# The engines' order around the context's last rows written out by hand, the transposes placed between the first products of two pairs, and the second matrix's sums put two pairs later

## The chip, the cores and the metric

One core of one Trainium2 chip runs the whole program. The metric is the device time of one execution in microseconds (us), given as the median over several runs.

## The reference

One layer of a backbone for 256 context tokens and 1024 latent tokens, model width 1024, in float32. The part that matters here is its second half, computed for both kinds of tokens:

```python
    x = x + gt1 * (merged @ w_out)
    u2 = rmsnorm(x, g_norm2) * (1 + sc2) + sh2
    x = x + gt2 * (jnp.square(jax.nn.relu(u2 @ w_ff1)) @ w_ff2)
```

`gt1`, `sc2`, `sh2` and `gt2` come from the conditioning vector (one for context tokens, one for latent ones), and `w_ff1` is 1024 x 4096, `w_ff2` 4096 x 1024.

## The kernel before, in words

All numbers are float32. A product of two float32 matrices is made of three matmuls: each operand is split into a high part, which ScalarE casts, and a low part, the rest, which VectorE subtracts; then high by high, low by high and high by low are summed in PSUM. Names that end in `h` and `l` (or begin with `hi_` and `lo_`) are these parts.

The tokens stand in tiles of 128: 0 to 3 are the first group of latent tokens (512), 4 to 7 the second, 8 and 9 the context (256). The steps around the change are:

- **The output projection.** `project_out(tiles, c0, n, ...)` multiplies `merged` by a stretch of `n` columns of `w_out`, 24 matmuls for a tile, and leaves the sum in a PSUM tile `po{c0}_{tile}`. VectorE multiplies it by `gt1` and adds it to x; ScalarE squares x and gathers the row sums in `fsq`. The context's tiles 8 and 9 go by quarters of 256 columns: `context_out(0)` to `context_out(3)`, with weights from `context_weights(q)` (tiles `hi_wc`, `lo_wc`).
- **The normalization.** `modulate_ff(g)` takes a group's row sums (`fs`), makes the reciprocal root (`rstd_of`: a small step on VectorE, then one on GpSimd, `rs_f`), scales x by it (tiles `xn`, the even ones on ScalarE, the odd ones on VectorE), transposes on TensorE into a PSUM tile (`pt2{g}_{k}`) and applies scale and shift on ScalarE. For groups 0 and 1 the result is `u2r{k}_{g}`, with its split `u2h`, `u2l`; for the context (g = 2) it goes back into the PSUM tile, and VectorE makes the split `u2{k}c` from it. These PSUM tiles share one pool of five (`ps_sd`) with the results of the products below.
- **The first matrix.** The 4096 columns of `w_ff1` are worked off in 16 pairs. For the latent tokens a pair is a 2 x 2 block product in the way of Strassen and Winograd, with seven products of 12 matmuls of 128x512 each. `begin()` splits two of the four weight quarters (`a11`, `a12`) and makes the first two products, `B11` and `B21` (PSUM `fB11_{pair}`, `fB21_{pair}`): ScalarE copies the first one twice, VectorE adds the second, and `done` is relu and square on ScalarE. `contexts()` makes the plain products for the context tokens (PSUM `fc{pair}`) with all four weight quarters. `rest()` makes the other five products (`T4`, `T2`, `T3`, `T1`, `B22`; PSUM `fT...`), whose operands are sums: on the side of the tokens `quarter_sums`, four subtractions for each of four rows, and their splits `split_sum`, both made once; on the side of the weights four sums for each pair, with the splits `s1` to `s4`. `sums()` stores the results.
- **The second matrix's sums.** `second_sums(fp)` loads a pair's block of `w_ff2` (SyncE's queue), makes four subtractions of 128x512 on GpSimd (L1242) and stores them in `scr_t`. The product with the second matrix, behind all 16 pairs, loads them from there.

The 16 latent transposed tiles of 128x512, `u2r0` to `u2r7` for two groups, are the operands of the products. Pairs 0 and 1 share `slot` tiles for their weights: `a21_0` goes into the room of `a11_0`, `a21_1` into that of `a11_1`, and so on, which sets when the later quarter can be split.

What sets the order: the program's text gives the instructions, and a scheduler with a timeline of its own reorders each engine's instructions when the program is built, within their dependencies; loads are reordered on SyncE's queue as well. An instruction that is issued through `Pinned` keeps its place in the written order among the pinned ones of its engine. On the chip each engine works off its instructions strictly in the built order. Before the change nothing in this part is pinned. Instructions issued through `Pinned` carry L43, the line of the wrapper.

The written order before is: `context_out(0)`, `context_out(1)`, `modulate_ff(1)`, `context_out(2)`, `context_out(3)`, then `begin()` of pairs 0 and 1, `modulate_ff(2)`, `quarter_sums`, the four `split_sum`, `contexts()` of both pairs, and for each pair its remaining steps with `second_sums` of the same pair at the end.

Of the kernel before, what the change touches and what calls it, by code (L numbers as in the profile page):

```python
# [48 lines left out]
def hybrid_step(  # L49
# [77 lines left out]
    def rstd_of(ssq, n, name):  # L127
        r = small([P, 16], f"rs_{name}")
        V.tensor_scalar(r[:, :n], ssq, 1.0 / n_of[name[0]], EPS, ALU.mult, ALU.add)  # L129
        G.tensor_tensor(r[:, :n], r[:, :n], neghalf[:, :n], ALU.pow)  # L130
        return r
# [738 lines left out]
    def split(raw, name, room=ring):  # L870
        hi, lo = room(f"{name}h"), room(f"{name}l")
        A.copy(hi, raw)
        V.tensor_tensor(lo, raw, hi.bitcast(F32), ALU.subtract)
# [20 lines left out]
    class Pair:  # L894
# [23 lines left out]

        def begin(self):
            a11, a12, a21, a22 = self.raw  # L920
            self.w11 = split(a11, f"a11_{self.name}", self.rooms[0])
            ps = self.prod(self.w11, "B11")
            A.copy(self.a1, ps)
            A.copy(self.a2, ps)
# [2 lines left out]
            V.tensor_tensor(self.a1, self.a1, ps, ALU.add)
# [317 lines left out]

# [290 lines left out]
```

## Time and profile before

| | |
|---|---|
| median of 3 runs | 1947.19 us (1946.92 to 1949.57) |
| profiled execution | 1947.31 us |
| its span in the trace | 1945.5 us, 28129 instructions |
| mean granted TensorE clock | 0.994 |
| TensorE busy | 1903.0 us, 98% of the span |
| VectorE, ScalarE, GpSimd busy | 1294.0, 861.7 and 378.2 us |
| chain that ended last | TensorE 87%, VectorE 4%, transfers 3%, GpSimd 2% |

Times of the trace are counted from the start of the span. A row of the timeline gives the start, the duration, the engine, the line, the operation, its output and its inputs with their shapes, the count of such instructions in one piece, and in square brackets the idle time ahead with the instruction that ended it. TensorE's matmuls overlap at their ends, so what one costs is the distance to the start of the next; the same holds, by less, for VectorE and ScalarE. In the trace buffer numbers are left out (`fB` stands for `fB11_0` and the others, `a_0l` for the low part of a weight quarter of pair 0), and which is meant follows from the order.

### The profile page before, as it was taken

What the parts mean: (1) busy time and instruction counts of PE and PEld (TensorE: products, weight loads), DVE (VectorE), ACT (ScalarE), POOL (GpSimd) and SP (SyncE); (2) the same over time, 40 slices, a digit from 0 to 9 for tenths busy, and PEclk for the clock granted to TensorE, in tenths of its full rate; (3) what the DMA queues carried; (4) which work ended last, traced back from release to release, by engine and by line L of the source; (5) the groups of instructions that cost most, each with busy time, mean ns of one, the idle gap of its engine ahead of it and who ended that gap; (6) DMA issues with size and microseconds to landing.
All of it is one profiled execution on the core that took longest, in us unless ns stands there. A gap on an engine that the chain in (4) does not pass through costs nothing.

```text
span 1945.5 us, 28129 instructions
## 1 busy us (share of the span) xinstructions
PE 1903.0 (98%) x10136; PEld 1627.5 (84%) x10136; DVE 1294.0 (67%) x2207; ACT 861.7 (44%) x1768; POOL 378.2 (19%) x380
## 2 busy tenths in 40 slices
PE   6999999999999999999999999999999999999998
PEld 3778888998788888888888887888888888888886
DVE  6574443347759889875675599888776655744665
ACT  7444464653243333343123374555454545443443
POOL 1200001107302424220000015444431110000003
PEclk9999999999999999999999999999999999999999
DMA  9211111012635445469522435776773586654444
GB/s 361 85 59 33 43 39 40 27 56 70 203 119 165 149 158 164 153 211 321 163 97 98 152 120 212 253 264 246 259 269 136 193 333 203 210 170 151 165 133 159
DMA packets 149318, 313.32 MB, mean 161 GB/s; under 512 B 17550, under 2 KB 40818, under 8 KB 147130
## 3 DMA queue, kind: packets, MB, share of 16 engines
q1 hardware_dynamic: 107354, 220.73, 33.9%
q0 software_dynamic: 15520, 57.75, 7.8%
q10 hardware_dynamic: 26304, 33.04, 4.7%
q8 instruction: 79, 1.29, 0.3%
q14 instruction: 61, 0.50, 0.1%
HBM read 217.59 MB, written 93.36 MB: 160 GB/s over the span
## 4 chain that ended last, share of the span: by engine, by line
PE 87%; DVE 4%; DMA 3%; POOL 2%; ACT 1%; issue 1%; SPq 0%; POOLq 0%; ACTq 0%; DVEq 0%
PE w L1403 6%; PE w L1404 6%; PE w L1405 6%; PE pb L1050 3%; PE pb L1051 3%; PE pb L1052 3%; PE fT L892 3%; PE fT L890 3%; PE fT L891 3%; PE fB L891 2%; PE fB L890 2%; PE fB L892 2%; PE fT_g L892 2%; PE fT_g L890 2%; PE fT_g L891 2%; PE po L1168 2%
## 5 line engine op out<-in xcount | busy, mean ns | idle before, releaser
L1242 POOL TENSOR_TENSOR z<-z 128x512 f32<-128x512 f32 x64 | 100.1, 1564 | 123.3 <-DMA z<-in_w_ff 120.6
L947 DVE TENSOR_TENSOR z<-z 128x512 f32<-128x512 f32 x112 | 88.7, 792 | 2.5
L527 POOL PARTITION_ALL_REDUCE acc<-acc x16 | 54.6, 3446 | 184.0 <-DVE acc L521 113.6
L521 DVE SCALAR_TENSOR_TENSOR acc<-z,scond,acc 128x512 f32<-128x512 f32 x112 | 86.1, 816 | 0.0
L1357 POOL TENSOR_TENSOR rs_y<-rs_y,neghalf 128x1 f32<-128x1 f32 x10 | 9.6, 966 | 333.0 <-DVE rs_y L1356 333.0
L1208 ACT ACTIVATE z<-z 128x512 f32<-128x512 f32 x64 | 40.5, 632 | 69.8 <-DVE z L956 36.7
L972 ACT ACTIVATE z<-z 128x512 f32<-128x512 f32 x48 | 30.3, 632 | 59.1 <-DVE z L956 23.1
L130 POOL TENSOR_TENSOR rs_h<-rs_h,neghalf 128x4 f32<-128x4 f32 (+1 forms) x12 | 10.9, 910 | 200.5 <-DVE rs_h L129 200.3
L653 DVE SCALAR_TENSOR_TENSOR yc<-th,ccol,z 128x512 f32<-128x512 f32 (+1 forms) x12 | 7.9, 661 | 58.2 <-PE th L651 58.2
L1056 DVE TENSOR_TENSOR sg<-pb,sg 128x512 f32<-128x512 f32 (+1 forms) x48 | 28.7, 600 | 26.7 <-PE pb L1052 26.5
L881 ACT CAST hi_wb<-raw_wb 128x512 fp32r<-128x512 f32 x24 | 14.8, 620 | 64.4 <-PE pb L1051 37.6
L1209 ACT ACTIVATE z<-z 128x512 f32<-128x512 f32 x64 | 40.3, 629 | 1.1
L1171 DVE TENSOR_TENSOR po<-po,gt 128x512 f32<-128x512 f32 (+1 forms) x24 | 14.6, 607 | 35.1 <-PE po L1170 35.0
L1233 POOL DMA_DIRECT2D scr_s<-x x48 | 26.3, 549 | 53.1 <-DVE x L1227 47.6
L738 POOL TENSOR_TENSOR z<-z 128x1024 f32<-128x1024 f32 (+13 forms) x20 | 33.6, 1702 | 6.9 <-ACT z L722 4.6
L528 POOL TENSOR_TENSOR acc<-acc,bt 1x512 f32<-1x512 f32 x16 | 23.5, 1480 | 58.4 <-issue 58.4
L1174 ACT ACTIVATE po<-z 128x512 f32<-128x512 f32 (+1 forms) x24 | 12.7, 529 | 48.5 <-DVE z L1173 34.2
L587 DVE SCALAR_TENSOR_TENSOR z<-z,dmb,kv 128x129 f32<-128x129 f32 x56 | 16.6, 345 | 21.8 <-PE kv L576 21.3
L1057 DVE TENSOR_TENSOR z<-z,sg 128x512 f32<-128x512 f32 (+1 forms) x48 | 28.7, 601 | 1.2
L640 DVE TENSOR_TENSOR den<-den,gcol 128x2 f32<-128x2 f32 x40 | 6.2, 159 | 31.0 <-ACT den L639 29.9
L43 PE MATMUL pm<-wah,shl 128*4 128x512 f32 x32 | 13.8, 461 | 13.2 <-ACT wah L43 13.2
L130 POOL TENSOR_TENSOR rs_f<-rs_f,neghalf 128x4 f32<-128x4 f32 (+1 forms) x3 | 3.3, 1092 | 116.9 <-DVE rs_f L129 116.9
(5136 smaller groups left out, 7288.9 us busy)
## 6 DMA issues: line engine op xcount, KB each, us to landing
z<-in_w_ff SPq DMA_DIRECT2D x64, 512.0 KB, 5.5
z<-in_w_ada SPq DMA_DIRECT2D x64, 256.0 KB, 3.1
scr_t<-z POOLq DMA_DIRECT2D x16, 1024.0 KB, 4.9
z<-in_w_in SPq DMA_DIRECT2D x24, 512.0 KB, 4.3
scr_g<-z ACTq DMA_DIRECT2D x48, 256.0 KB, 2.0
sg<-scr_g SPq DMA_DIRECT2D x48, 256.0 KB, 4.5
scr_h<-z ACTq DMA_DIRECT2D x48, 256.0 KB, 3.6
scr_s<-x POOLq DMA_DIRECT2D x48, 256.0 KB, 4.3
```

The lines of the kernel that those rows point to most:

```text
L521: V.scalar_tensor_tensor(acc[j], raw, scond[:, k, j : j + 1], acc[j], ALU.mult, ALU.add)
L890: PE.matmul(ps, whi[:, s], ahi, start=first and k == ks[0], stop=False)
L891: PE.matmul(ps, whi[:, s], alo, start=False, stop=False)
L892: PE.matmul(ps, wlo[:, s], ahi, start=False, stop=end and k == ks[-1])
L947: V.tensor_tensor(out, x, y, op)
L1050: PE.matmul(pb[:, :n], whi[:, s], yh, start=kc == 0, stop=False)
L1051: PE.matmul(pb[:, :n], whi[:, s], yl, start=False, stop=False)
L1052: PE.matmul(pb[:, :n], wlo[:, s], yh, start=False, stop=kc == 3)
L1242: G.tensor_tensor(out, x, y, ALU.subtract)
L1403: PE.matmul(banks[j], h_[:, s], rh, start=fp == 0, stop=False)
L1404: PE.matmul(banks[j], l_[:, s], rh, start=False, stop=False)
L1405: PE.matmul(banks[j], h_[:, s], rl, start=False, stop=fp == NFP - 1)
```

## The change

1. `context_out(2)`, `context_out(3)` and all that follows up to the split of the sums is issued through `Pinned`: VectorE, ScalarE, GpSimd and TensorE keep the written order. The weights of both quarters, the feeds of the pairs 0 and 1 and their splits are issued ahead or between, unpinned.
2. `begin()` is cut into `split_first`, `first` and `second`, and `modulate_ff` into `root_ff` and the quarters to be done. The written order now is: first product of pair 0, second product of pair 0, first quarter of the context's rows (transposes `pt22_0`, `pt22_1`), first product of pair 1, second quarter, second product of pair 1, and the last two quarters.
3. The rows of `quarter_sums` (now `row_sums(kk)`) stand one by one among these steps, pinned on VectorE. The split sums are pinned on VectorE as well, in the order T4, T2, T3, T1.
4. SyncE's loads of the pair loop are pinned, and `second_sums` of a pair is written behind the steps of the pair two later; the last two stand behind the loop.
5. In the product with the second matrix, the order of the places that take the first raw loads (`FREE`) changes.

```diff
+        def first(self):
+            ps = self.prod(self.w11, "B11")
+            A.copy(self.a1, ps)
+            A.copy(self.a2, ps)
+
+        def second(self):
+            ps = self.prod(self.w12, "B21")
+            V.tensor_tensor(self.a1, self.a1, ps, ALU.add)
+            self.done(self.a1)
...
+    def row_sums(kk):
+        b11, b21, b12, b22 = (raw2q[nm][kk] for nm in ("B11", "B21", "B12", "B22"))
+        for out, x, y in ((b11, b12, b11), (b12, b22, b12), (b22, b22, b11), (b21, b22, b21)):
+            V.tensor_tensor(out, x, y, ALU.subtract)
...
     for fp in (0, 1):
         feed_pair(fp)
-        pairs[fp].begin()
-    modulate_ff(2)
-    quarter_sums(raw2q)
-    for nm in ("T4", "T3", "T2", "T1"):
+    wcs = [context_weights(q) for q in (2, 3)]
+    V, A, G, PE = (Pinned(tc, e) for e in engines)
+    context_out(2, wcs[0])
+    row_sums(0)
+    context_out(3, wcs[1])
+    P4, (V, A, G, PE) = (V, A, G, PE), engines
+    for fp in (0, 1):
+        pairs[fp].split_first()
+    V, A, G, PE = P4
+    rc = root_ff(2)
+    row_sums(1)
+    pairs[0].first()
+    pairs[0].second()
+    modulate_ff(2, rc, (0,))
+    pairs[1].first()
+    modulate_ff(2, rc, (1,))
+    row_sums(2)
+    pairs[1].second()
+    modulate_ff(2, rc, (2, 3))
+    A, G, PE = engines[1:]
+    row_sums(3)
+    for nm in ("T4", "T2", "T3", "T1"):
         split_sum(u2s, raw2q, nm)
+    V = engines[0]
     for fp in (0, 1):
         pairs[fp].contexts()
+    SP = Pinned(tc, nc.sync)
     for fp in range(NFP):
...
         del pairs[fp]
-        second_sums(fp)
+
+        if fp > 1:
+            second_sums(fp - 2)
+    second_sums(NFP - 2)
+    second_sums(NFP - 1)
+    SP = nc.sync
...
-    FREE = (0, 2, 16, 18, 12, 14, 4, 6, 8, 10)
+    FREE = (0, 2, 12, 14, 16, 18, 4, 6, 8, 10)
```

Three places of the built order show what moves.

**The front, on TensorE.** Between the second and the third quarter of the context's projection stand the transposes of `modulate_ff(1)`; `pt21_{k}` is transposed tile k of the second latent group, `xn4` and `xn6` are its even tiles of scaled rows by quarter. Before, its tile 6 stands among the last matmuls of `po512_8`:

```order
L1170 MATMUL po512_8_10722<-lo_wc2_3_10719,m6c_9782 128x256
L1168 MATMUL po512_8_10722<-hi_wc2_3_10718,m7c_9785 128x256
L1142 MATMUL pt21_6_10676<-cst_76,xn4_3_10670 128x128 x2
L1169 MATMUL po512_8_10722<-hi_wc2_3_10718,m7c_9785 128x256
L1170 MATMUL po512_8_10722<-lo_wc2_3_10719,m7c_9785 128x256
L1142 MATMUL pt21_6_10676<-cst_76,xn6_3_10673 128x128 x2
L1168 MATMUL po512_9_10750<-hi_wc2_0_10700,m0c_9764 128x256
```

After the change tiles 5, 6 and 7 stand with the others, ahead of the first matmul of `po512_8`:

```order
L1158 MATMUL pt21_5_10659<-cst_76,xn4_2_10642 128x128 x2
L1158 MATMUL pt21_5_10659<-cst_76,xn6_2_10645 128x128 x2
L1158 MATMUL pt21_6_10676<-cst_76,xn4_3_10670 128x128 x2
L1158 MATMUL pt21_6_10676<-cst_76,xn6_3_10673 128x128 x2
L1158 MATMUL pt21_7_10687<-cst_76,xn4_3_10670 128x128 x2
L1158 MATMUL pt21_7_10687<-cst_76,xn6_3_10673 128x128 x2
L43 MATMUL po512_8_10806<-hi_wc2_0_10760,m0c_9764 128x256 x2
```

What moved is the last three tiles' transposes: all of them now come before the third quarter's first product.

**The context's first quarter, on ScalarE and VectorE.** `fB11_0`, `fB21_0` and `fB11_1`, `fB21_1` are the first two products of pairs 0 and 1, `xn8_{q}` the scaled context rows by quarter, and the `z` rows between are the copies, relu and square of a pair. ScalarE before:

```order
L923 COPY z_74<-fB11_1_10963 128x512
L924 COPY z_74<-fB11_1_10963 128x512
L1174 ACTIVATE po768_8_10802,fsq_9815<-z_74 128x256
L1174 ACTIVATE po768_9_10831,fsq_9815<-z_74 128x256
L1208 ACTIVATE z_74<-z_74 128x512
L1209 ACTIVATE z_74<-z_74 128x512
L1221 DMA scr_h0_10860<-z_74 128x512
L1208 ACTIVATE z_74<-z_74 128x512
L1209 ACTIVATE z_74<-z_74 128x512
L1221 DMA scr_h1_10861<-z_74 128x512
L1134 ACTIVATE xn8_0_11003<-z_74,rs_f2_11000 128x256
L1134 ACTIVATE xn8_1_11020<-z_74,rs_f2_11000 128x256
```

ScalarE after:

```order
L43 ACTIVATE po768_8_10866,fsq_9815<-z_74 128x256
L43 COPY z_74<-fB11_0_10949 128x512 x2
L43 ACTIVATE po768_9_10895,fsq_9815<-z_74 128x256
L43 ACTIVATE z_74<-z_74 128x512 x2
L43 ACTIVATE xn8_0_10980<-z_74,rs_f2_10942 128x256
L1234 DMA scr_h0_10698<-z_74 128x512
L43 ACTIVATE pt22_0_10983<-pt22_0_10983,sh2_9799,a2_9798 128x256
L43 ACTIVATE pt22_1_10990<-pt22_1_10990,sh2_9799,a2_9798 128x256
L43 COPY z_74<-fB11_1_10997 128x512 x2
L43 ACTIVATE xn8_1_11012<-z_74,rs_f2_10942 128x256
L43 ACTIVATE pt22_2_11015<-pt22_2_11015,sh2_9799,a2_9798 128x256
L43 ACTIVATE pt22_3_11022<-pt22_3_11022,sh2_9799,a2_9798 128x256
```

The first quarter `xn8_0` now stands behind relu and square of pair 0 alone and ahead of the copies of pair 1's first product; before, all four quarters stood behind both pairs. VectorE before:

```order
L927 TENSOR_TENSOR z_74<-z_74,fB21_0_10941 128x512
L780 TENSOR_TENSOR u2r6_0_10333<-u2r6_1_10681,u2r6_0_10333 128x512
L790 TENSOR_TENSOR t2l2_11128<-u2r6_1_10681,t2h2_11127 128x512
L780 TENSOR_TENSOR u2r7_1_10692<-u2r7_1_10692,u2r3_0_10288 128x512
L1122 TENSOR_REDUCE fs2_10998<-fsq_9815 128x2
L927 TENSOR_TENSOR z_74<-z_74,fB21_1_10982 128x512
L780 TENSOR_TENSOR u2r7_0_10344<-u2r7_1_10692,u2r7_0_10344 128x512
L129 TENSOR_SCALAR rs_f2_11000<-fs2_10998 128x2
L1136 TENSOR_SCALAR xn8_0_11003<-z_74,rs_f2_11000 128x256
```

VectorE after:

```order
L43 TENSOR_REDUCE fs2_10940<-fsq_9815 128x2
L43 TENSOR_SCALAR rs_f2_10942<-fs2_10940 128x2
L43 TENSOR_TENSOR u2r1_0_10260<-u2r1_1_10620,u2r1_0_10260 128x512
L43 TENSOR_TENSOR u2r1_1_10620<-u2r5_1_10664,u2r1_1_10620 128x512
L43 TENSOR_TENSOR u2r5_1_10664<-u2r5_1_10664,u2r1_0_10260 128x512
L43 TENSOR_TENSOR u2r5_0_10316<-u2r5_1_10664,u2r5_0_10316 128x512
L43 TENSOR_TENSOR z_74<-z_74,fB21_0_10964 128x512
L43 TENSOR_SCALAR xn8_0_10980<-z_74,rs_f2_10942 128x256
```

Before, the row sums that lie around the small steps `fs2` and `rs_f2` are the last rows of the quarter sums; now row 1 as a whole stands between `rs_f2` and the addition of `fB21_0`, and rows 2 and 3 come later. On TensorE `pt22_0` and `pt22_1` now follow the last matmul of `fB21_0`, with `fB11_1` behind them; before, `pt22_0` followed `fB21_1`.

**Pair 1's second product and the context's third quarter, on ScalarE.** `a21_0h` is the high part of pair 0's third weight quarter, `pt22_{k}` the scale and shift of a transposed context tile, `T4h0` the first split of the sums. Before:

```order
L1146 ACTIVATE pt22_5_11047<-pt22_5_11047,sh2_9799,a2_9798 128x256
L1146 ACTIVATE pt22_6_11057<-pt22_6_11057,sh2_9799,a2_9798 128x256
L1146 ACTIVATE pt22_7_11064<-pt22_7_11064,sh2_9799,a2_9798 128x256
L789 CAST T4h0_11087<-u2r4_0_10305 128x512
L872 CAST a21_0h_11179<-z_74 128x512
L789 CAST T4h1_11091<-u2r5_0_10316 128x512
```

After:

```order
L43 ACTIVATE pt22_3_11022<-pt22_3_11022,sh2_9799,a2_9798 128x256
L872 CAST a21_0h_11179<-z_74 128x512
L43 ACTIVATE z_74<-z_74 128x512 x2
L43 ACTIVATE xn8_2_11049<-z_74,rs_f2_10942 128x256
L1234 DMA scr_h1_10699<-z_74 128x512
L43 ACTIVATE pt22_4_11052<-pt22_4_11052,sh2_9799,a2_9798 128x256
L43 ACTIVATE pt22_5_11059<-pt22_5_11059,sh2_9799,a2_9798 128x256
```

`a21_0h` stood behind all eight context tiles; now it stands ahead of relu and square of pair 1 and of `xn8_2`.

More of the change, by code (lines that the diff above doesn't have):

```diff
@@ L917, in context, with split_first @@
                 self.context_done(self.hc[:, f * 256 : f * 256 + 256], o)
+        def split_first(self):
+            a11, a12, a21, a22 = self.raw
+            self.w11 = split(a11, f"a11_{self.name}", self.rooms[0])
+            self.w12 = split(a12, f"a12_{self.name}", self.rooms[1])
+        def first(self):
[6 more added lines that the diff above has]
+            self.done(self.a1)
         def begin(self):
@@ L921, in begin @@
             self.w11 = split(a11, f"a11_{self.name}", self.rooms[0])
-            ps = self.prod(self.w11, "B11")
-            A.copy(self.a1, ps)
-            A.copy(self.a2, ps)
+            self.first()
             self.w12 = split(a12, f"a12_{self.name}", self.rooms[1])
-            ps = self.prod(self.w12, "B21")
-            V.tensor_tensor(self.a1, self.a1, ps, ALU.add)
-            self.done(self.a1)
+            self.second()
         def contexts(self):
@@ L1116, in hybrid_step, with root_ff @@
     fsq = cp.tile([P, NT, 4], F32, name="fsq")
-    def modulate_ff(g):
+    def root_ff(g):
         t0, n = GROUPS[g]
@@ L1122, in modulate_ff @@
         V.reduce_sum(fs, fsq[:, tiles[0] : tiles[-1] + 1, 0 : 4 if g == 2 else 2], axis=mybir.AxisListType.X)
-        r = rstd_of(fs, len(tiles), f"f{g}")
+        return rstd_of(fs, len(tiles), f"f{g}")
+    def modulate_ff(g, r=None, quarters=range(4)):
+        t0, n = GROUPS[g]
+        tiles = range(t0 // P, (t0 + n) // P)
+        r = root_ff(g) if r is None else r
         j = 1 if g == 2 else 0
-        for qt in range(4):
+        for qt in quarters:
             xn = []
@@ L1176, in project_out, with context_out @@
                 SP.dma_start(scr_x[i], xt[i])
-    def context_out(q):
-        ws = context_weights(q)
+    def context_out(q, ws):
         project_out((8, 9), q * 256, 256, lambda k: tuple(w[:, k % 2 * 256 : k % 2 * 256 + 256] for w in ws[k // 2]))
@@ L1188, in hybrid_step @@
     project_out(range(5, 8), 512, 512, lambda k: w_out1[k])
-    context_out(0)
-    context_out(1)
+    for q in (0, 1):
+        context_out(q, context_weights(q))
     modulate_ff(1)
@@ L1193, in hybrid_step @@
     raw2q = {nm: raw2[g][o : o + 4] for nm, g, o in quarters}
-    context_out(2)
-    context_out(3)
     NFP = NFF // 2
```

## The prediction

> **What bounds the kernel now.** I read the first lines of the page, then TensorE's own waits from 1080 to 1620 us (the stretch that the diff touches), then busy time by stretch.
>
> ```profile
> span 1945.5 us, 28129 instructions
> PE 1903.0 (98%) x10136; PEld 1627.5 (84%) x10136; DVE 1294.0 (67%) x2207; ACT 861.7 (44%) x1768; POOL 378.2 (19%) x380
> PE pt L1142 <- ACT xn L1134: 3.0, 1, 3.0
> PE fT L890 <- ACT s_0h L872: 0.9, 3, 0.4
> PE fT L892 <- DVE s_2l L873: 0.9, 1, 0.9
> PE fc L890 <- ACT hc L1212: 0.7, 1, 0.7
> PE fT L890 <- ACT s_2h L872: 0.7, 1, 0.7
> PE w L1403 <- ACT r_13h L1302: 0.5, 1, 0.5
> 1150.00:1160.00 10.00, 6.97 (x31) 5.58 (x30) 8.24 (x19) 6.35 (x15) 0.70 (x1) 0.94 0.39 158
> 1170.00:1180.00 10.00, 8.94 (x59) 7.61 (x57) 10.00 (x18) 7.01 (x16) 2.50 (x3) 1.00 0.64 228
> 1210.00:1220.00 10.00, 9.22 (x51) 7.34 (x49) 7.15 (x14) 5.06 (x10) 2.62 (x5) 1.00 0.97 345
> 1220.00:1230.00 10.00, 8.43 (x51) 7.22 (x50) 9.93 (x13) 5.27 (x12) 7.79 (x8) 1.00 0.62 221
> 1230.00:1560.00 330.00, 330.00 (x1746) 285.31 (x1745) 246.49 (x364) 169.57 (x314) 118.33 (x135) 1.00 0.65 233
> ```
>
> TensorE works in 1903.0 of 1945.5 us, so it is the bound. A wait row is what waited, for whom, the sum, the count and the longest. The six rows come to 6.7 us: the change can hardly win more here than that and the little lost at a low clock. In the window rows (span, then PE, PEld, DVE, ACT, POOL, granted clock, DMA share) TensorE is full from 1230 on, and VectorE is full from 1170 to 1180. Here VectorE is a second bound, and whatever makes VectorE idle before 1190 comes out again as TensorE's wait.
>
> The one large wait, 3.0 us, is for `xn8_0`, the normalized last context rows. Its chain:
>
> ```profile
> 1153.88 0.59 ACT L924 COPY z<-fB 128x512 f32<-128x512 f32 x1
> 1154.77 0.39 ACT L1174 ACTIVATE po<-z 128x256 f32<-128x256 f32 x1
> 1155.17 0.62 ACT L1208 ACTIVATE z<-z 128x512 f32<-128x512 f32 x1
> 1155.83 0.63 ACT L1209 ACTIVATE z<-z 128x512 f32<-128x512 f32 x1
> 1158.56 1.71 ACT L1134 ACTIVATE xn<-z,rs_f 128x256 f32<-128x256 f32 x4 [0.40 <-POOL rs_f L130]
> 1156.12 0.69 DVE L927 TENSOR_TENSOR z<-z,fB 128x512 f32<-128x512 f32 x1 [0.38 <-PE fB L892]
> 1156.72 0.68 DVE L780 TENSOR_TENSOR u2r<-u2r,u2r 128x512 f32<-128x512 f32 x1
> 1157.33 0.16 DVE L129 TENSOR_SCALAR rs_f<-fs 128x2 f32<-128x2 f32 x1
> 1157.57 0.70 POOL L130 TENSOR_TENSOR rs_f<-rs_f,neghalf 128x2 f32<-128x2 f32 x1 [33.16 <-DVE rs_f L129]
> 1145.01 0.40 PE L890 MATMUL fB<-u2h,a_0h 128*128 128x512 f32 x1
> 1155.69 0.39 PE L892 MATMUL fB<-u2h,a_1l 128*128 128x512 f32 x1
> 1159.12 2.39 PE L1142 MATMUL pt<-cst,xn 128*128 128x128 f32 x10 [3.03 <-ACT xn L1134]
> ```
>
> All four first products of pairs 0 and 1 run together from 1145.01 to 1155.92 (48 matmuls between these two rows, 0.227 apart, so 2.73 a product). TensorE idles 3.03 us, and only then come the transposes.
>
> **The change, part by part: the front.** Before, the last three transposed tiles of `modulate_ff(1)` lie among the projection's matmuls; now they all stand ahead of `po512_8`.
>
> ```profile
> 1130.03 2.35 PE L1142 MATMUL pt<-cst,xn 128*128 128x128 f32 x20
> 1132.13 0.36 PE L1168 MATMUL po<-hi_wc,m0c 128*128 128x256 f32 x1
> 1134.40 0.78 ACT L1151 ACTIVATE u2r<-pt,sh,a 128x512 f32<-128x512 f32 x1
> 1144.77 0.28 PE L1169 MATMUL po<-hi_wc,m7c 128*128 128x256 f32 x1
> 1144.89 0.28 PE L1170 MATMUL po<-lo_wc,m7c 128*128 128x256 f32 x1
> ```
>
> Twenty transposes take 2.10 (1130.03 to 1132.13), four 0.35 or so. They fill the five tiles at hand; the last three wait until ScalarE has emptied tiles, the third with `u2r2`, which ends at 1135.18. So `po512_8` starts at about 1135.6, not 1132.13. Then its four products of 24 matmuls, 0.12 apart (1144.77, 1144.89), run undisturbed: 11.5 us, to 1147.1. Before it was 1145.01: **+2.1**.
>
> **First stall.** Pair 0's two products end at 1147.1 + 5.45 = 1152.6, and TensorE's next instruction is `pt22_0`, which needs `xn8_0`. By the rows above: `fB11_0` is in at 1150.1; two copies at 0.48 (0.59 with the end) to 1151.1; the square of `po768_9`, on which the row sum depends, 0.5 to 1151.6; the reduction and `rs_f2` 0.3 to 1151.9; GpSimd's 0.70 to 1152.7. VectorE meanwhile has `row_sums(1)`, four at 0.60 (1156.72 to 1157.33 is one such step), written ahead of the addition of `fB21_0`: to 1154.4. The addition ends at 1155.1, relu and square (0.66 each, 1155.17 to 1155.83) at 1156.4, and only behind these on ScalarE stands `xn8_0`, at 0.4: 1156.8. TensorE idles 4.2. It then stands at 1156.85 with two products of four done; the other two at 5.45 make it equal to 1162.3 of before, where this point was 1159.12: **a lag of 3.2**.
>
> **Second stall.**
>
> ```profile
> 1168.15 0.62 ACT L872 CAST a_0h<-z 128x512 fp32r<-128x512 f32 x1 [0.56 <-PE fc L891]
> ```
>
> `pt22_0`, `pt22_1` 0.4, `fB11_1` 2.73, twelve context matmuls 1.44: 1161.4. `xn8_1` stands behind the two copies of `fB11_1` (1161.6), `pt22_2`, `pt22_3` to 1162.0, `fB21_1` to 1164.8, twelve matmuls to 1166.25. `pt22_4` needs `xn8_2`, which on ScalarE stands behind `a21_0h`, relu and square of pair 1. The new wait is that of `a21_0h`: it overwrites `a11_0h`, which TensorE's context products of `u23c` read until 1166.0. Before, such a cast had the same wait, 0.56 (1168.15), but stood behind everything on ScalarE that made `xn8`. Behind it now: the cast 0.62 to 1166.65; on VectorE `a21_0l` and the last of `row_sums(2)` at 0.60, and the addition, to 1168.6; relu, square and `xn8_2` to 1170.45. TensorE idles 4.2 again. Without the wait at `a21_0h` the addition starts at 1164.9, `xn8_2` is ready at about 1167.4, and this stall is 1.1; so that one wait is worth 3.
>
> **Behind it.**
>
> ```profile
> 1163.50 0.54 ACT L1146 ACTIVATE pt<-pt,sh,a 128x256 f32<-128x256 f32 x1 [0.40 <-PE pt L1142]
> 1164.82 0.41 DVE L1147 CAST u26c<-pt 128x256 fp32r<-128x256 f32 x1
> 1180.95 0.68 DVE L873 TENSOR_TENSOR s_0l<-z,s_0h 128x512 fp32r<-128x512 f32 x1
> 1181.69 0.50 PE L892 MATMUL fT<-t2h,s_0l 128*128 128x512 f32 x1 [0.30 <-DVE s_0l L873]
> 1167.52 1.77 DVE L873 TENSOR_TENSOR a_0l<-z,a_0h 128x512 fp32r<-128x512 f32 x1
> 1164.37 6.08 POOL L1242 TENSOR_TENSOR z<-z 128x512 f32<-128x512 f32 x4 [6.10 <-DMA z<-in_w_ff]
> 1178.57 13.34 POOL L1242 TENSOR_TENSOR z<-z 128x512 f32<-128x512 f32 x4 [7.20 <-DMA z<-in_w_ff]
> ```
>
> VectorE and ScalarE set the pace: `pt22_4` takes 0.4 on TensorE and 0.54 on ScalarE, to 1171.4; the cast and the dependent subtraction of `u24c` on VectorE end at 1172.05, those of `u25c` at 1172.85 (each 0.41); VectorE's half of `xn8_3` 0.33, transposes and ScalarE again to 1173.95; `u26c` 1174.8, `u27c` 1175.6. Then 22 operations at 0.60 and two short ones up to `s2_0l`, 13.6: it ends at about 1189.3. Before, its counterpart ended at 1181.63 (1180.95 and 0.68), and TensorE ran the matmul on it at 1181.69: **a lag of 7.7**. The late `second_sums` have their gain in this already: while GpSimd subtracts, VectorE's 128x512 operations take up to 1.77 (1167.52) where alone they take 0.68 (1180.95), about 3 us lost in the 6.08 from 1164 alone, an estimate from two such operations and three more behind them. The walk has none of this. If GpSimd's work had stayed, the lag would be 3 more.
>
> **Clock.**
>
> ```profile
> 1160.00:1161.00 1.00, 1.00 (x7) 1.00 (x6) 0.29 (x1) 1.00 (x3) 0.00 (x0) 0.50 0.29 82
> 1163.00:1164.00 1.00, 1.00 (x11) 1.00 (x10) 1.00 (x4) 0.60 (x2) 0.00 (x0) 1.00 0.60 246
> ```
>
> The granted clock falls to 0.50 after the idle 3.03 us and is back by 1163; the ten transposes then take 2.07 (1159.12 to the next matmul) instead of 1.05. Two idles of 4.2 can each do the same. Behind the first stands a whole product, so about 1.5 us are lost there; behind the second little, since VectorE sets the pace. Between 0 and 3 for both; I take 1.2, near the one loss that this trace shows. [...]
>
> **Behind 1192.** The second sums now run two pairs late and SyncE's loads are pinned in their written order. The three later waits (`s_2h`, `hc`, `s_2l`: 2.3 together, the gaps of the windows from 1210 to 1230) lie behind GpSimd's and SyncE's work, which the change moves. Bounds: all three go (-2.3) or none does and `a11_2h` comes late in the pinned queue (+1). I take -1.2. From 1230 on TensorE has no gap in 330 us to give, so neither late sums nor the order of `FREE` can win there; what they can touch behind that stretch is the 0.5 at `r_13h`, which may go or grow: 0, plus or minus 1.
>
> **Sum.** 7.7 + 1.2 - 1.2 = +7.7 on the profiled execution's 1947.31 (the span and 1.8 around it; the median of the runs is 1947.19, the same within 0.01%): **1955.0 us**.
>
> **Rivals.** 0.2%, 3.9 us, is about what a measurement of this kernel can tell from no change, so faster is below 1943.3 and slower above 1951.1.
> - *The transposes are hidden: faster, 1939 to 1943.* This holds if `xn8_0` is ready when `fB21_0` ends (1152.6) and `xn8_2` when the context's twelve matmuls end. Then the 3.03 idle, the 1.5 of clock and up to 2.3 behind go, against the front's +2.1: 1947.3 - 6.8 + 2.1 = 1942.6, or 1940.5 if the front's 2.1 is taken up by the wait that goes. For it: GpSimd's losses do go. Against it: four row sums and a relu and a square stand ahead of `xn8_0`; it decides at 1152.6, and my walk misses it by 4. Chance 0.17.
> - *The lag is caught up: 1946 to 1951.* If the wait at `a21_0h` is short (the cast finds its room free), the second stall is 1.1, the lag falls to 4.7, and the later waits go: 1947.3 + 4.7 - 2.3 = 1949.7. Chance 0.13.
> - *Worse than the walk: 1958 to 1963.* Both stalls cost a half clock at full price (+3) and pair 2's weights come late in the pinned queue (+1 to +2) with none of the later waits gone: 1947.3 + 7.7 + 3 + 1.5 = 1959.5. Chance 0.15.
> - *The pins don't hold the order:* the built order shows them in place, so I give this nothing.
>
> **How the numbers follow.** The walk has 0.55, by itself 1951 to 1958; with the worse case, slower has 0.70, same 0.13, faster 0.17. The range goes from 1942.0 to 1961.0: the deeper half of the hidden case and the far end of the worse one, some 0.15 together, are left out.
>
> **What would show it.** Right: two TensorE waits on `pt22_0` and `pt22_4` of about 4 us each, `po512_8` some 3.5 us later than before, an idle VectorE from 1155 to 1175, and 1.77 gone from its 128x512 operations up to 1195. Wrong: transposes that follow `fB21_0` without a gap; a short wait at `a21_0h`; or a gap behind 1230 that the first stage does not explain.

## The result, and the profile after

| | before | after |
|---|---|---|
| median of 4 runs each | 1948.38 us (1946.92 to 1950.46) | 1967.57 us (1965.55 to 1969.30) |
| profiled execution, its span | 1947.31, 1945.5 us | 1967.77, 1966.0 us |
| mean granted TensorE clock | 0.994 | 0.992 |
| chain that ended last: TensorE, VectorE, transfers | 87%, 4%, 3% | 81%, 7%, 5% |

The ratio after to before is 1.0097, with a 95% interval from 1.0085 to 1.0109: the change makes the kernel slower by 1%. The predicted 1955.0 us has the right sign, but the time lies above the range that ended at 1961.0.

The first question is where the 20.5 us of span came from. The two executions reach the changed stretch 0.6 us apart, so I divide the span at two marks: the first of the transposes of `modulate_ff(1)`, and the first matmul on `w`, with which the product with the second matrix begins. TensorE's timeline gives them, the changed kernel's first:

```profile
1130.60 2.78 PE L1158 MATMUL pt<-cst,xn 128*128 128x128 f32 x24
1567.62 0.50 PE L1447 MATMUL w<-r_0h,l_0h 128*128 128x512 f32 x1
```

and the second mark of before (its first mark, 1130.03, stands in the prediction):

```profile
1556.23 0.39 PE L1403 MATMUL w<-r_0h,l_0h 128*128 128x512 f32 x1
```

From mark to mark (stage A: the last context rows and the 16 pairs) it is 437.0 us instead of 426.2, so 10.8 more. From the second mark to the end (stage B: the second matrix) it is 1966.0 - 1567.62 = 398.4 instead of 389.3, so 9.1 more. The remaining 0.6 lies ahead of both. **About half of the loss thus lies in a stage for which the prediction had 0, plus or minus 1.**

The largest of TensorE's waits of the changed kernel from 1080 to 1640 us (what waited, for whom, sum, count, longest) and all of `w` show both halves:

```profile
PE pt L43 <- ACT xn L43: 8.5, 3, 4.3
PE w L1447 <- ACT r_13h L1346: 2.0, 1, 2.0
PE w L1447 <- ACT accU L1411: 1.6, 1, 1.6
PE w L1447 <- ACT l_4h L1346: 1.5, 1, 1.5
PE w L1448 <- DVE c_0l L1347: 0.5, 1, 0.5
PE w L1447 <- ACT r_12h L1346: 0.3, 1, 0.3
```

The wait for `xn` has grown from 3.0 to 8.5, and five waits of `w` with 5.9 us stand where before there was one of 0.5. The busy time by stretch of the same kernel (span, then PE, PEld, DVE, ACT and POOL busy, granted clock, DMA share, GB/s):

```profile
1150.00:1160.00 10.00, 5.66 (x22) 4.47 (x21) 5.66 (x14) 4.50 (x11) 1.07 (x1) 0.86 0.33 132
1160.00:1170.00 10.00, 8.61 (x49) 7.23 (x47) 5.15 (x11) 3.09 (x6) 0.00 (x0) 0.97 0.00 0
1170.00:1180.00 10.00, 5.70 (x27) 4.90 (x28) 4.58 (x12) 4.60 (x9) 0.00 (x0) 0.66 0.07 26
1190.00:1200.00 10.00, 7.53 (x23) 5.09 (x23) 10.00 (x20) 5.57 (x11) 0.57 (x1) 0.83 0.09 26
1210.00:1560.00 350.00, 350.00 (x1859) 302.83 (x1858) 284.87 (x389) 176.44 (x328) 141.70 (x150) 1.00 0.63 233
1600.00:1605.00 5.00, 2.64 (x9) 1.04 (x8) 3.72 (x7) 3.21 (x6) 0.00 (x0) 0.93 0.91 344
1605.00:1610.00 5.00, 5.00 (x18) 4.04 (x18) 4.44 (x8) 4.73 (x9) 1.08 (x2) 0.72 0.65 206
```

In the stretches from 1150 to 1180 VectorE, ScalarE and GpSimd idle together with TensorE: nobody is short of time there, each waits for the next in a chain. From 1190 to 1200 VectorE is full: it works off what was put back. From 1210 to 1560 TensorE is full again. Behind 1600, in stage B, it loses 2.4 us, and its clock falls for some 3 us (0.72 from 1605 to 1610).

The two stalls, on TensorE's timeline:

```profile
1157.43 1.11 PE L43 MATMUL pt<-cst,xn 128*128 128x128 f32 x4 [4.34 <-ACT xn L43]
1172.77 1.11 PE L43 MATMUL pt<-cst,xn 128*128 128x128 f32 x4 [4.00 <-ACT xn L43]
1174.54 0.58 PE L890 MATMUL fc<-u24c,a_0h 128*128 128x256 f32 x1 [0.66 <-DVE u24c L43]
1177.48 0.59 PE L43 MATMUL pt<-cst,xn 128*128 128x128 f32 x3
1194.57 0.66 PE L892 MATMUL fT<-t2h,s_0l 128*128 128x512 f32 x1 [0.74 <-DVE s_0l L873]
```

They are 4.34 and 4.00 us long, where the prediction had 4.2 and 4.2, and what VectorE and ScalarE did ahead of the second one is what it said: `a_0h` waits for TensorE, and addition, relu, square and `xn` follow it one after the other. The cast on ScalarE:

```profile
1168.45 0.62 ACT L872 CAST a_0h<-z 128x512 fp32r<-128x512 f32 x1 [3.07 <-PE fc L891]
```

### The profile page after: what moved, and what is told of

Its sections match the earlier page's. It is cut to its first block, busy times and chain, and to the rows that moved or that the text cites. A ratio compares the mean times of both kernels' runs of the same rounds, so it can differ in the third digit from the quotient of the medians.

```text
span 1966.0 us, 28101 instructions
## 1 busy us (share of the span) xinstructions
PE 1910.3 (97%) x10136; PEld 1630.4 (83%) x10136; DVE 1314.3 (67%) x2207; ACT 861.8 (44%) x1768; POOL 378.7 (19%) x380
## 4 chain that ended last, share of the span: by engine, by line
PE 81%; DVE 7%; DMA 5%; ACT 3%; issue 2%; POOL 1%; SPq 0%; POOLq 0%; DVEq 0%; ACTq 0%
PE w L1447 5%; PE w L1449 5%; PE w L1448 5%; PE fT L892 3%; PE fT L890 3%; PE fT L891 3%; PE pb L1062 3%; PE pb L1061 3%; PE pb L1063 3%; PE fB L891 2%; PE fB L892 2%; PE fB L890 2%; PE po L1184 2%; PE po L1185 2%; PE po L1186 2%
## 5 line engine op out<-in xcount | busy, mean ns | idle before, releaser
L958 DVE TENSOR_TENSOR z<-z 128x512 f32<-128x512 f32 x112 | 110.8, 989 | 2.5
L1244 POOL DMA_DIRECT2D scr_c<-xc x16 | 11.6, 726 | 131.5 <-DVE xc L1243 131.5
```

The lines of the kernel that those rows point to most:

```text
L958: V.tensor_tensor(out, x, y, op)
```

## The experiments

Every table entry comes from its kernel's profiled execution, except the ratio, which compares the runs with those of before on the same chip (95% interval in brackets). The forecasts call the kernels by names: experiments 1 to 12 are there e1, e2, e3, e5, e7, e6, e8, e9, e13, e12, e14 and e15.

| kernel | stage A | stage B | ratio |
|---|---|---|---|
| before | 426.2 | 389.3 | 1 |
| the change | 437.0 | 398.4 | 1.0097 [1.0085, 1.0109] |
| 1: order by hand, sums as before | 450.1 | 389.5 | 1.0111 [1.0089, 1.0133] |
| 2: late sums, order as before | 419.9 | 397.4 | 1.0005 [0.9994, 1.0016] |
| 3: 1 with `a21_0` behind | 450.9 | 389.9 | 1.0117 [1.0102, 1.0132] |
| 4: 3 with the rows first | 446.7 | 393.6 | 1.0102 [1.0081, 1.0123] |
| 5: the change, front as before | 435.2 | 396.5 | 1.0079 [1.0060, 1.0099] |
| 6: 2 with sums that catch up | 419.9 | 389.5 | 0.9968 [0.9956, 0.9980] |
| 7: the change, all rows early | 422.5 | 397.3 | 1.0022 [1.0012, 1.0032] |
| 8: 7 with sums that catch up | 423.8 | 390.6 | 0.9984 [0.9974, 0.9994] |
| 9: the change with sums that catch up | 437.2 | 389.4 | 1.0046 [1.0030, 1.0062] |
| 10: 8 with three steps moved | 426.4 | 389.4 | 1.0001 [0.9992, 1.0010] |
| 11: 6 again | 421.0 | 389.3 | 0.9961 [0.9948, 0.9975] |
| 12: the change, other places | 436.3 | 400.8 | 1.0107 [1.0085, 1.0128] |

Stage B takes 389.3 to 390.6 in every kernel whose last second sums are done early, but for the fourth, and 396.5 to 400.8 in every kernel where they are late. In stage A the sixth kernel differs from its own repeat by 1.1 (419.9 and 421.0): behind the same stall of 3.0 us the clock was halved for about 3.4 us in the sixth and for about 6.8 in the repeat, an estimate from windows of 10 us (from 1150 and from 1160 the clock is 0.99 and 0.83 in the sixth, 0.87 and 0.79 in the repeat). So a difference of about 1 us in this table is not read as an effect.

**1 and 2: the change in its two halves.** The first keeps the order by hand and puts the second sums back:

```diff
-    SP = Pinned(tc, nc.sync)
     for fp in range(NFP):
...
-        if fp > 1:
-            second_sums(fp - 2)
-    second_sums(NFP - 2)
-    second_sums(NFP - 1)
-    SP = nc.sync
+        second_sums(fp)
...
-    FREE = (0, 2, 12, 14, 16, 18, 4, 6, 8, 10)
+    FREE = (0, 2, 16, 18, 12, 14, 4, 6, 8, 10)
```

> The hand-written order of the change alone; the second matrix's sums, SyncE's order and FREE as before. Theory A (two separate losses: the order costs about 12 between 1130 and 1200, the late sums cost about 9 at the start of the second matrix's product): 1957 to 1960 us, stalls of about 4 at pt22_0 and pt22_4 as in the change, and the waits behind 1560 (5.9 us) gone. Theory B (the late sums cost nothing, as the prediction had it; the waits behind 1560 come from the late arrival out of the first stage): 1965 to 1968 us with those waits still there.

The second is before with only the late sums, the pinned loads and the new `FREE` (the same lines the other way).

> The kernel before, with only the sums two pairs late, SyncE pinned in the pair loop and the new FREE. Theory A: 1953 to 1957 us, waits of 5 to 8 us in the product w, none new between 1130 and 1560, VectorE free of GpSimd between 1164 and 1191. Theory B: 1945 to 1949 us.

The first took 1972.80 us, more than either theory gave, and through a wait that neither had. Among its TensorE waits, and then SyncE's largest wait from 1150 to 1240:

```profile
PE fc L890 <- ACT a_2h L872: 6.9, 1, 6.9
```

```profile
SPq L1252 <- DMA scr_t<-z: 28.6, 3, 13.6
```

and SyncE's queue, where L1252 are the loads of the second sums and L905 those of the pairs' weights:

```profile
1202.55 0.33 SPq L905 DMA_DIRECT2D z<-in_w_ff  x1
1216.59 0.80 SPq L1252 DMA_DIRECT2D z<-in_w_ff  x2
1217.45 11.77 SPq L905 DMA_DIRECT2D z<-in_w_ff  x3
```

Its window from 1160 to 1240 (columns as above):

```profile
1160.00:1240.00 80.00, 64.53 (x281) 52.25 (x281) 59.41 (x97) 35.70 (x69) 33.30 (x22) 0.82 0.43 154
```

The same stretch of the changed kernel, of before and of the second experiment, in this order:

```profile
1160.00:1240.00 80.00, 71.48 (x364) 60.02 (x363) 66.09 (x109) 41.71 (x81) 19.43 (x21) 0.93 0.38 140
```

```profile
1160.00:1240.00 80.00, 75.56 (x397) 63.22 (x396) 74.12 (x113) 43.83 (x85) 39.39 (x31) 0.99 0.63 226
```

```profile
1160.00:1240.00 80.00, 79.56 (x431) 69.12 (x430) 69.47 (x116) 48.29 (x93) 25.51 (x26) 0.98 0.52 180
```

The order by hand makes TensorE idle for 15.5 us of these 80 and lowers its clock (0.82 over these 80, 0.54 from 1220 to 1230). Pair 2's first weight load goes out at 1202.55, about when it does in the changed kernel (1201.56). Its second one, which `a_2h` needs, goes out only at 1217.45: on the queue it stands behind two loads of the second sums, and the first of these waited 13.6 us until a store of earlier sums had freed its place. With the late sums the idle time falls to 8.5, in the old order from 4.4 to 0.4. In stage A the late sums win 13.1 us in the new order (450.1 to 437.0) and 6.3 in the old one (426.2 to 419.9); the order by hand costs 23.9 without them and 17.1 with them. "Late sums" is a bundle here: the sums come two pairs later and SyncE's loads are pinned. Which of the two wins in stage A, no run parted. In the second experiment the waits in stage B appear at once (2.0 at `r_13h`, 1.1 at `l_4h`, 0.8 at `r_4h`, 0.7 at `r_12h`; 4.6 together, and a clock of 0.91 from 1560 to 1600), stage B is 8.1 longer, and its 1950.99 us is no change.

**3 and 4: which wait makes the second stall.** The prediction held that the wait of `a21_0h` is worth 3 us. The third kernel pins its split behind the last context rows, on top of the first:

```diff
     modulate_ff(2, rc, (2, 3))
+    pairs[0].w21 = split(pairs[0].raw[2], "a21_0", pairs[0].rooms[2])
     A, G, PE = engines[1:]
```

> As e1, but the split of a21_0 stands behind pt22_7 on ScalarE and VectorE. If the wait of a21_0h makes the second stall: pt22_4's stall falls from 4.0 to about 1 and the time is 3 to 5 us under e1. If VectorE's pace sets the end of this stretch whatever TensorE does: the stall goes but the time is within 1 us of e1.

The second stall fell from 4.00 to 3.03, and the time stayed (1974.12 us). The wait was worth 1, not 3: with the cast gone, the four steps of `row_sums(2)` still stand ahead of the addition on VectorE.

The fourth puts the first quarter's rows ahead of `row_sums(1)`, the addition and relu, and the last two ahead of pair 1's addition:

```diff
-    row_sums(1)
     pairs[0].first()
-    pairs[0].second()
+    pairs[0].second_product()
     modulate_ff(2, rc, (0,))
+    row_sums(1)
+    pairs[0].second_done()
     pairs[1].first()
     modulate_ff(2, rc, (1,))
     row_sums(2)
-    pairs[1].second()
+    pairs[1].second_product()
     modulate_ff(2, rc, (2, 3))
+    pairs[1].second_done()
```

> As e3, and the context's quarters stand ahead of row_sums(1) and ahead of addition, relu and square of their pair, behind the products on TensorE. If what stands ahead of xn8_0 makes the first stall: pt22_0's stall falls from 4.3 to about 1, no half clock follows, and the time is 1945 to 1951 us. If the transposes between the products are no better than behind them (VectorE's pace): within 2 us of e3.

TensorE's timeline of it:

```profile
1152.61 0.66 PE L43 MATMUL pt<-cst,xn 128*128 128x128 f32 x4 [0.57 <-ACT xn L43]
1161.45 1.11 PE L43 MATMUL pt<-cst,xn 128*128 128x128 f32 x4 [4.02 <-ACT xn L43]
```

The stall at `pt22_0` falls from 4.34 to 0.57, so the steps written ahead of `xn8_0` made it. But one quarter later the same stall stands at `pt22_2`, since the row sums, the addition, relu, square and two copies now lie ahead of `xn8_1`. It was moved, not removed (1970.69 us). Stage B has 4 us more here than the others with early sums; 2.4 of it is a wait for the eviction `accU`, whose cause I did not follow.

**5: the front.** The third quarter's projection is not pinned on TensorE:

```diff
     V, A, G, PE = (Pinned(tc, e) for e in engines)
+    P4, PE = (V, A, G, PE), engines[3]
     context_out(2, wcs[0])
+    PE = P4[3]
```

> The whole change, but context_out(2) is not pinned on TensorE, so that the last transposes of modulate_ff(1) may lie among its matmuls again. If the front's loss of 2.1 is carried to the end: 1965 to 1966 us (2 under the change). If the stalls behind it take it up: within 0.7 of the change, 1967 to 1968.

Stage A is 1.8 shorter (437.0 to 435.2), where the prediction priced the front at 2.1. The 1.9 that stage B and the 0.4 that the part ahead of the marks have less are not the front's. The median, 1963.84 us, is 3.7 below the change's and so below both forecasts, by that shorter stage B, whose cause is open.

**6 and 11: are the late sums late at the end?** The second experiment, but with sums that lag at first and catch up by pair 13:

```diff
-        if fp > 1:
-            second_sums(fp - 2)
-    second_sums(NFP - 2)
-    second_sums(NFP - 1)
+        for s in {2: (0,), 3: (1,), 4: (2,), 5: (3, 4), 6: (5,), 7: (6, 7), 8: (8,), 9: (9, 10),
+                  10: (11,), 11: (12, 13), 12: (14,), 13: (15,)}.get(fp, ()):
+            second_sums(s)
```

> As e2 (the order of before, sums late), but the sums catch up: from pair 5 on every second pair issues two, so that the last stands behind pair 13. Theory C (what the late sums lose in the product w is that the last two sums still hold the places of its first raw loads): w begins at about 1550 as in e2, its waits fall from 4.6 us and a half clock to under 1, 1940 to 1943 us. Rival (the pinned loads or the new FREE delay w, not the lateness): 1946 to 1951 us with the waits still there.

1943.17 us: the gain in stage A stays (419.9) and the loss in stage B is gone (389.5). The pinned loads and the new `FREE` are those of the second, so in stage B it was the lateness that cost. Its TensorE waits of the whole stretch are three:

```profile
PE pt L1142 <- ACT xn L1134: 3.0, 1, 3.0
PE w L1407 <- ACT r_13h L1306: 0.6, 1, 0.6
PE fT L890 <- ACT a_0h L872: 0.4, 1, 0.4
```

This is the fastest version of the study. It was run once more (experiment 11):

> e6 again, unchanged, beside e12 on the same chip: 1940 to 1944 us.

It gave 1941.43 us, a ratio of 0.9961.

**7 and 8: transposes between the products, without the stalls.** On top of the fifth, all four quarters of `xn8` come right behind the root, ahead of pair 0's addition; the transposes stand behind the third product and among the context's products, and `a21_0` behind them. The eighth adds the sums that catch up.

```diff
     pairs[0].first()
-    pairs[0].second()
-    modulate_ff(2, rc, (0,))
+    pairs[0].second_product()
+    rows = scaled_rows(rc)
+    pairs[0].second_done()
+    row_sums(1)
     pairs[1].first()
-    modulate_ff(2, rc, (1,))
-    row_sums(2)
-    pairs[1].second()
-    modulate_ff(2, rc, (2, 3))
+    modulate_ff(2, rc, (0, 1), rows)
+    pairs[1].second_product()
+    modulate_ff(2, rc, (2, 3), rows)
+    pairs[1].second_done()
+    row_sums(2)
+    pairs[0].w21 = split(pairs[0].raw[2], "a21_0", pairs[0].rooms[2])
```

> The whole change with its late sums, but all four quarters of xn8 are made as soon as the root is there, ahead of additions, relu and row sums; the transposes stand behind the third and among the context's products; a21_0 behind them; front as in e7. If what stood ahead of xn8 on ScalarE and VectorE made the stalls: no TensorE wait over 1.2 between 1140 and 1180, w begins at 1550 to 1554, 1946 to 1952 us. If VectorE's pace holds the lag whatever the stalls: w begins near 1560, 1957 to 1962 us.

> e8 with the sums of e6. If both theories hold, their gains add: 1936 to 1943 us. If only one holds: 1946 to 1957 us.

The seventh has no wait for `xn` at all, and its stage A is 422.5, which is 14.6 below the change's and 12.7 below the fifth's (435.2), on which it builds. So transposes between the products need not cost what they cost in the change. Whether the other order on VectorE and ScalarE wins this or the place of the transposes, one product later on TensorE, was not parted. And 422.5 is no better than the 419.9 of the second experiment, which keeps the 3.0 at `xn`. The seventh's largest wait has moved to the sums on the side of the weights, as its timeline shows:

```profile
1179.88 0.50 PE L892 MATMUL fT<-t2h,s_0l 128*128 128x512 f32 x1 [2.35 <-DVE s_0l L873]
```

VectorE is full from 1170 to 1190 there (19.9 of 20 us): in this order too its work sets when `s_0l` is there. The eighth, 1946.08 us, gets stage B back but not what the sixth has in stage A.

**9: the whole change with sums that catch up.** The edit is that of the sixth, on the changed kernel.

> The whole change with the sums of e6 (they catch up), nothing else. If the lateness of the last sums is what the change loses in the product w (9 us by its trace): w begins near 1567 as in the change, its waits fall from 5.9 to about 1, 1957 to 1961 us. If the waits there come from the first stage's lag: 1965 to 1968.

1958.79 us, 8.8 below the change: stage A stays at 437.2, stage B falls from 398.4 to 389.4.

**10: an order nearer to the free one.** On top of the eighth, the row sums 0 and 1 are left to the scheduler, 2 and 3 stand behind `xn8`, and `a21_0` ahead of relu.

```diff
-    row_sums(0)
+    V = engines[0]
+    row_sums(0)
+    row_sums(1)
+    V = P4[0]
     context_out(3, wcs[1])
...
     pairs[0].second_done()
-    row_sums(1)
+    row_sums(2)
...
-    pairs[1].second_done()
-    row_sums(2)
     pairs[0].w21 = split(pairs[0].raw[2], "a21_0", pairs[0].rooms[2])
-    A, G, PE = engines[1:]
     row_sums(3)
+    pairs[1].second_done()
+    V, A, G, PE = engines
```

> e9 with two rows of the quarter sums free to fill VectorE's idle time ahead of 1150, the other two behind xn8, and a21_0 ahead of pair 1's relu. If what e9 lacks against e6 is VectorE's idle time from 1130 to 1140 under the pins: under e6, 1936 to 1942 us. If pins cost elsewhere: 1943 to 1947.

It missed, with 1948.70 us. A new wait stands further ahead, at the last quarter of the projection:

```profile
1148.50 0.80 PE L43 MATMUL po<-hi_wc,m0c 128*128 128x256 f32 x2 [3.71 <-ACT po L43]
```

The row sums now lie ahead of the steps that empty the projection's PSUM tiles, and pinned TensorE waits.

**12: is it the place that blocks the queue?** The changed kernel with the places of the last second sums (16 to 19) at the end of `FREE`:

```diff
-    FREE = (0, 2, 12, 14, 16, 18, 4, 6, 8, 10)
+    FREE = (0, 2, 12, 14, 4, 6, 8, 10, 16, 18)
```

> The whole change, but with the two places that the last second sums use (16 and 18) last in FREE: (0, 2, 12, 14, 4, 6, 8, 10, 16, 18). It parts two readings of the 9 us that the change loses behind the first matmul on w, where from that matmul to the end it takes 398.4 us against 389.3 before. Theory A, the blocked queue: the fifth raw load into place 16 stands on SyncE's queue for 9.2 us until the store of the last second sums has landed, and what is behind it comes late; with the place last in the order nothing else stands behind that wait but the loads of the ninth and tenth pairs, so the stretch falls to 390 to 393, the waits at l_4h and r_13h go to below 1.0 together, and the median is 1959 to 1962. Theory B, the late sums themselves (GpSimd busy until 1567, its stores and loads shared): the order of the places does nothing, the stretch stays at 396 to 400 and the median at 1965 to 1969. A mixed case: places 4 to 10, free only when pair 15 is done, are late as well, and the stretch is 393 to 396.

This kernel doesn't part the theories. On SyncE's queue the scheduler left the load into place 16 where it was, directly behind `r_10r`; only the pair that it serves is another, and four raw loads of this kind are issued from there on in both kernels. SyncE's waits from 1550 to 1610 in it:

```profile
SPq L1355 <- DMA scr_t<-z: 9.7, 1, 9.7
```

So the block stayed, and stage B stayed with it (400.8). The wait at `l_4h` gave way to one of 3.8 at `r_6h`, whose raw load stands behind the block. But ahead of the cast `r_6h` on ScalarE stands one of `c_2r`, and this one's load, issued at 1580.95, took 10.4 us to land:

```profile
1591.42 0.62 ACT L1346 CAST c_2h<-c_2r 128x512 fp32r<-128x512 f32 x1 [12.02 <-DMA c_2r<-scr_c]
```

That fits a blocked queue, and it fits transfers that are slow because there are many of them (the DMA share is 1.03 from 1560 to 1600); which of the two it was is not shown. Late sums with a free queue were not measured.

## Why the prediction was right about the sign and wrong about the size

**The front: right.** Predicted +2.1; with it undone stage A falls by 1.8.

**The first stall: right.** Predicted 4.2, measured 4.34. With two products of 5.45 us still to come, `pt22_0` at 1157.43 equals 1162.88 of before, against 1159.12; less the 0.57 by which this execution began the stretch later, the lag is 3.2, the predicted figure.

**The second stall: right in its size, wrong in one of its causes.** Predicted 4.2, measured 4.00, with the chain that was named. But "that one wait is worth 3" (of `a21_0h`) was mis-sized: taken away, it gave 1.0, because the row sums ahead of the addition were still there.

**The clock: mis-sized.** The term was 1.2 for both stalls, with "behind the second little, since VectorE sets the pace". The windows behind the second stall and behind 1194:

```profile
1174.00:1175.00 1.00, 0.46 (x2) 0.46 (x3) 0.90 (x3) 0.91 (x3) 0.00 (x0) 0.50 0.00 0
1176.00:1177.00 1.00, 1.00 (x6) 1.00 (x6) 0.00 (x0) 0.00 (x0) 0.00 (x0) 0.50 0.00 0
1177.00:1178.00 1.00, 1.00 (x7) 0.84 (x5) 0.00 (x0) 0.10 (x1) 0.00 (x0) 0.66 0.00 0
1194.00:1195.00 1.00, 0.43 (x1) 0.36 (x2) 1.00 (x2) 0.00 (x0) 0.00 (x0) 0.88 0.00 0
1195.00:1196.00 1.00, 1.00 (x4) 0.78 (x3) 1.00 (x4) 0.25 (x1) 0.00 (x0) 0.50 0.00 0
```

Here VectorE did not set the pace. From 1176 to 1178 TensorE is full and VectorE idle: the transposes `pt22_6` (its second half) and `pt22_7` stand behind the twelve context matmuls of `u24c` and `u25c`, which the walk left out, and these take 2.94 at half clock (1174.54 to 1177.48), twice the 1.44 that the prediction gave twelve of them at the first stall. `u27c`, predicted for 1175.6, ended at 1180.13 (1179.56 without the later start). Of the 4.0 between, about 1.8 was there at `pt22_4` already (1172.20 without the later start, against 1170.45): the half clock behind the first stall (0.50 from 1158 to 1160), where `pt22_0`, `pt22_1` and the product `fB11_1` took 4.74 (1157.43 to 1162.17) instead of 0.4 and 2.73, 1.6 more. The other 2.2 is the step left out. At `s_0l` the lag was 1194.57 - 1181.69 - 0.57 = 12.3, against 8.9 (7.7 and the clock's 1.2). That is the 7.7, about 1.8, 2.2 and another 0.7: the stretch of VectorE from `u27c` to `s_0l` took 14.4 instead of 13.6, with 23 long operations in it and not 22. Both stalls halved the clock (0.50 from 1158 to 1160 and from 1171 to 1177), as the 3.03 of before did (0.50 from 1159 to 1162); behind the 4.02 of experiment 4 it is 0.67 from 1160 to 1170. The shorter waits for `s_0l` went both ways: behind the 2.35 of experiment 7 the clock is 1.00 from 1180 to 1190, behind the 2.37 of experiment 8 it is 0.83 there. Behind the changed kernel's first stall 1.6 were lost so and behind the second 1.5 (2.94 for 1.44), together 3.1 where the term had 1.2 in a range from 0 to 3.

**Behind 1192: near, and partly by luck.** Predicted -1.2. The lag went from 12.3 there to 10.8 at the first matmul on `w`, so -1.5. But all three later waits are gone, which was the bound of -2.3, and a stretch at half clock that was not foreseen (0.50 from 1195 to 1198) gave part of it back. In the old order the late sums (with the pinned loads) win 6.3 in stage A, close to the 6.7 of all waits that the prediction named as the most there was to win.

**The late sums behind 1230: the step that failed most.** The prediction said that "neither late sums nor the order of `FREE` can win there; what they can touch behind that stretch is the 0.5 at `r_13h`, which may go or grow: 0, plus or minus 1". It asked only what a full TensorE could win, not what late loads and stores could hold up behind it. Its own sign of being wrong, "a gap behind 1230 that the first stage does not explain", came true. The changed kernel's largest wait of SyncE from 1550 to 1600, its queue around that wait, and GpSimd's last second sums:

```profile
SPq L1355 <- DMA scr_t<-z: 9.2, 1, 9.2
```

```profile
1564.33 0.33 SPq L1355 DMA_DIRECT2D r_10r<-in_w_ff  x1
1573.96 0.33 SPq L1355 DMA_DIRECT2D z<-in_w_ff  x1
1597.32 0.33 SPq L1355 DMA_DIRECT2D r_13r<-in_w_ff  x1
```

```profile
1564.16 2.67 POOL L1255 TENSOR_TENSOR z<-z 128x512 f32<-128x512 f32 x2
1567.12 0.58 POOL L1256 DMA_DIRECT2D scr_t<-z  x1 [0.30 <-POOL z L1255]
```

GpSimd ends the last pair's four subtractions at 1566.8, and their store is issued at 1567.12. The next raw load overwrites their place and must wait for that store, 9.2 us, and SyncE issues nothing else in that time. `r_13r` is issued 29.7 us behind the first matmul on `w`, against 23.7 before (its row there is 1579.93, below). Before, the scheduler had drawn the last sums ahead, and their last store was issued at 1438.8. The row of `r_13r` of before:

```profile
1579.93 0.33 SPq L1311 DMA_DIRECT2D r_13r<-in_w_ff  x1
```

That lateness of the last sums costs the 9.1 is shown from both sides: late sums without the order by hand bring it into the old order (397.4), and catching up takes it out of the old (389.5) and of the new order (389.4). How it costs that, these rows alone don't settle. Before, SyncE stands still at the same place too, for 6.8 us, behind `r_10r`. But there the raw loads of the first steps are ahead of it: `r_4h` is cast at 1556.74, 0.5 behind the first matmul on `w`, and in the changed kernel 13.7 behind it, after a wait for its load:

```profile
1581.26 0.62 ACT L1346 CAST r_4h<-z 128x512 fp32r<-128x512 f32 x1 [6.20 <-DMA z<-in_w_ff]
```

The other explanation is the amount of transfers. The late sums bring their loads and stores into the time in which the product's raw loads are due. From 40 us ahead of the first matmul on `w` to 25 behind it the changed kernel moves 21.7 MB, before 17.9. The 25 us behind that matmul and the 10 behind these, first of the changed kernel and then of before (columns as above):

```profile
1567.62:1592.62 25.00, 23.04 (x100) 18.37 (x100) 13.20 (x22) 10.95 (x19) 9.55 (x18) 1.00 1.03 389
1592.62:1602.62 10.00, 9.08 (x38) 6.66 (x36) 5.28 (x8) 4.68 (x8) 0.00 (x0) 1.00 1.03 401
1556.23:1581.23 25.00, 25.00 (x112) 20.72 (x111) 15.02 (x25) 12.16 (x23) 6.04 (x12) 1.00 1.04 406
1581.23:1591.23 10.00, 9.45 (x42) 7.37 (x41) 5.59 (x10) 5.51 (x11) 1.05 (x2) 1.00 0.52 185
```

The DMA engines are full in both, but in the changed kernel for about 10 us longer; while SyncE waits (1564.66 to 1573.96) they are busy at 0.93. At 400 GB/s the 3.9 MB more take some 10 us, an estimate from these rows, which is as much as stage B lost. So whether the load that waits or the amount of transfers makes the loss is open: no run removed the block and kept the lateness.

**The sum.** Predicted +7.7: 7.7 of lag, 1.2 of clock and -1.2 behind. Measured in the profiled execution: 10.8 in stage A, so 3.1 above the forecast, from what the half clock took beyond the term, the step left out and VectorE's 0.7, less 0.3 that came better than forecast behind 1192; 9.1 in stage B, for which 0 had been taken; 0.6 ahead of both. The excess, 3.1 + 9.1 + 0.6 = 12.8, is that of the profiled 1967.77 over 1955.0.

With the sums catching up (experiment 9, 1958.79 us) the time lies inside the predicted range, so the part of the forecast that left the range is stage B.

**The rivals.** *Worse than the walk* gave 1959.5 through a late pair 2 and a fuller price of the clock. Its half on the clock came true, its half on pair 2 did not: that wait (6.9 at `a_2h`) appears only where the sums are not late. *The transposes are hidden* needed `xn8_0` by 1152.6; it came 4.3 late, as the walk said.

**What stays open.** Through which of the two, queue or transfers, the late sums cost stage B; and why the early rows (experiments 7, 8 and 10) don't add to the gain of the sixth: each order took away the 3.0 at `xn` and lost as much at another place, and none was found that takes it away for nothing.

## What to carry to other kernels

Work that is put off so that it disturbs less must be back in time for the end of its loop: count what it still holds there (places, a store that has to land), what stands on the queue behind the first load that waits for it (SyncE issued nothing else for 9.2 us here), and the bytes it moves where the DMA engines are already full (1.03 here). To move a consumer ahead on one engine gains only if every step that feeds it is moved on its own engine as well; where they are not, the stall comes back one step later, as experiment 4 shows. And when a walk through a new order finds an idle time of TensorE like the stalls here (3.03, 4.00 and 4.34 us, each followed by a clock of 0.50), walk on at half clock, through every instruction in the queue and not only those on the chain.

## What the runs showed of the hardware that was not expected

The granted clock stayed at 0.50 from 1171 to 1177 although TensorE worked again from 1172.77 on, with short waits (0.66 at `u24c`). It fell again at about 1194.8, where no idle time had been longer than 1.1 us, but TensorE had been busy for less than half of the 4 us from 1191 to 1195:

```profile
1191.00:1192.00 1.00, 0.20 (x1) 0.00 (x0) 1.00 (x3) 1.00 (x3) 0.00 (x0) 1.00 0.03 8
1192.00:1193.00 1.00, 0.71 (x2) 0.30 (x2) 1.00 (x3) 1.00 (x3) 0.00 (x0) 1.00 0.84 254
1193.00:1194.00 1.00, 0.53 (x2) 0.19 (x1) 1.00 (x3) 0.80 (x2) 0.00 (x0) 1.00 0.00 0
```

So at this place the clock fell behind several short waits in a row, as it fell behind the long ones: it is 0.50 from 1195 to 1198, and the matmul of 128x512 that starts at 1194.57 stands with 0.66 in the timeline, where the same one of before, at 1181.69 and a clock of 1.00, stands with 0.50.
